# An encoder trunk on one core: C tables loaded behind three quarters of the scan inputs, first weights on ACT's queue, the gelu table load and the third in-chunk product moved in their queues

## The chip, the core and the metric

One core of a Trainium2 chip runs the whole program. The metric is device time in microseconds for one execution, the median of the runs. TensorE is PE in the rows, Vector DVE, Scalar ACT, GpSimd POOL; SP issues most of the DMAs, ACT some.

## The reference, cut to what matters

Two layers of an encoder over 512 tokens of width 1024, float32. Layer 0 mixes tokens with a bidirectional diagonal state-space model, layer 1 with a gated short convolution; each layer then attends into 256 memory tokens and applies a squared-ReLU MLP. The change lies wholly in layer 0's mixer:

```python
u = (h @ w_in)                         # 64 groups of 16 channels
y = d * u
for r in range(2):                     # two directions
    a_bar = exp(lam * dt)              # 64 states per group, complex
    bu = einsum('gph,lbgh->lbgp', b_bar, u)
    states = scan(x[l] = a_bar * x[l-1] + bu[l])
    y = y + einsum('ghp,lbgp->blgh', c, states).real
z = gelu(y); z = z * sigmoid(z @ w_glu); out = z @ w_out
```

## The kernel before, in words

The dense products of the program run as three float32r products on TensorE, fed by a stream of 1 MB weight blocks. Ahead of them, up to some 217 us of 1466, stands the mixer of layer 0, which is scheduled by hand: between `tc.manual_schedule()` and its end each engine executes its instructions in the order in which the code names them, so the order of the calls is the order of each queue.

The 512 tokens are cut into 64 chunks of 8. The mixer then has these steps, with the helper that holds each:

- `win_mm` (L683): u = x times `a_w_in`, four blocks of 256 columns. The loop at L253 to L258 loads x in four pieces (`xp`) and the first weight block in four pieces (`win[0]`), by turns on SP; ACT scales each x piece by the norm's gain (L276). `u_evac` (L690, L692) multiplies by the norm's factor on DVE, writes to DRAM and reads it back as `U` in the chunk layout.
- `sf_step`, `sf_transpose` (L518, L519): tables that carry a chunk's inputs into the state, eight of them (two per block of u), made on DVE, transposed on TensorE, copied by ACT to `sf`. They need the B tables `bf`.
- `s_mats` (L532, L534), eight calls, the "scan inputs": U times sf on TensorE, copied by ACT into `estate`, the state array of 64 chunk ends.
- `c_load` (L271): two transfers of 512 KB, the real and imaginary C tables `cf[0]` and `cf[1]`, on SP, and a page for their sum. `act.mul(cf[1], cf[1], -1.0)` (L747) negates the imaginary one on ACT. `q_tables` then forms the sum `cs` of both on DVE, and `q_ops` the eight Q tables (five DVE instructions each), which carry states to outputs.
- `scan_run`: the 62 scan steps on DVE, four small instructions a step, the last four Q tables woven between the first steps.
- `strips` (L556 to L576), four calls: in-chunk weights from Q and C tables on TensorE, copied by ACT (L570, L571), written to DRAM and read back by eight transfers as `mt` on SP. `y_intra(i)` (L586) is the in-chunk product of quarter i: U times mt. `y_carry` (L593) adds Q times the carried state.
- `p_part` (L673, L674): copies the states from `estate` into `pt`, for y_carry, in three portions as the scan goes on: chunks 0 to 26 and 26 to 46 on ACT, the rest mostly on DVE.
- `kvp(n)` runs n of the matmuls that make the memory's keys (L646) and values (L648) for layer 0. They fill TensorE while DVE scans; ACT copies the results (L658, L662). Their eight weight blocks are loaded on ACT's queue (four) and on SP's.

Pages of 4 KB a partition come from one pool of 30 (`page`): a new tile takes the buffer of a released one and waits for that one's last reader.

ACT loads its table of functions twice here: for the square root at the start (L89) and for gelu (L808), each with a one-column activation that fetches it ahead of its use.

Of the kernel before, what the change touches and what calls it, by code (L numbers as in the profile page):

```python
# [15 lines left out]
AF = mybir.ActivationFunctionType  # L16
# [30 lines left out]
def tile_encoder(ctx, tc, xT, xN, memT, memN, small, b_re, b_im, c_re, c_im, a_w_in, a_w_glu,  # L47
                 a_w_out, b_w_in, b_w_out, x_w_q, x_w_kv, x_w_o, f_w1, f_w2, out):
    nc = tc.nc
    v = nc.vector  # L50
    act = nc.scalar
# [15 lines left out]
    def nm(s):  # L67
        uid[0] += 1
        return f"{s}_{uid[0]}"

    def page(shape, dt=F32, name="pg"):
        return pgpool.tile([P] + list(shape), dt, tag="pg", name=nm(name))

    def bank(shape, name="ps"):
        return pspool.tile([P] + list(shape), F32, tag="ps", name=nm(name))
# [10 lines left out]
    epsb = cpool.tile([P, 1], F32, name="epsb")  # L86
    nc.gpsimd.memset(epsb, EPS)
    warm = cpool.tile([P, 1], F32, name="warm")
    act.activation(warm, epsb, AF.Sqrt)  # L89

    def gain(vec, k):
        o = OFF_G + vec * KT + k
        return sm[:, o:o + 1]
# [4 lines left out]
    def wblock(w, c0, k0=0):  # L98
        return w[k0 * P:(k0 + KT) * P, c0:c0 + 256].rearrange("(k p) m -> p k m", p=P)
# [152 lines left out]
    win = [stpool.tile([P, KT, 256], F32, tag="st", name=nm("st"))]  # L252
    w0 = wblock(a_w_in, 0)  # L253
    for kp in range(4):
        xp = xbig[:, 2 * kp:2 * kp + 2, :]
        nc.sync.dma_start(out=xp, in_=xT[256 * kp:256 * kp + 256, :].rearrange("(k p) n -> p k n", p=P))
        nc.sync.dma_start(out=win[0][:, 2 * kp:2 * kp + 2, :], in_=w0[:, 2 * kp:2 * kp + 2, :])
        hn.append(xp)  # L258
    bf = [page([G, 16], F32, "bf") for _ in range(2)]
    nc.sync.dma_start(out=bf[0], in_=b_re)  # L260
# [5 lines left out]
    cf = []  # L266

    def c_load():
        for src in (c_re, c_im):
            cf.append(page([G, 16], F32, "cf"))  # L270
            nc.sync.dma_start(out=cf[-1], in_=src)  # L271
        cf.append(page([G, 16], F32, "cs"))

    for k in range(KT):
        xk = hn[k // 2][:, k % 2, :]
        act.activation(xk, xk, AF.Copy, scale=gain(G_MIX, k))  # L276
# [35 lines left out]
    def tt(o, a, b, op):  # L312
        v.tensor_tensor(out=o, in0=a, in1=b, op=op)  # L313
# [139 lines left out]
    def q_tables():  # L453
        tt(dd, sm[:, OFF_D:OFF_D + 16].unsqueeze(2).to_broadcast([P, 16, 16]),
           sm[:, OFF_PAT:OFF_PAT + 16].unsqueeze(1).to_broadcast([P, 16, 16]), ALU.mult)
        tt(eq2[0], eq[:, 1], eq[:, 0], ALU.subtract)
        tt(eq2[1], eq[:, 0], eq[:, 1], ALU.add)
        tt(cf[2], cf[0], cf[1], ALU.add)
# [37 lines left out]
    def sf_gen(b):  # L496
        res, ops = gen_ops(b, bf, bs, es, [es2[:, 0], es2[:, 1]], False, "sfT")
        run_ops(ops)
        sfT[b] = res

    def bb_copy(b):
        res = sfT[b]
        for ri in range(2):
            o = bb[:, ri, 128 * b:128 * b + 128].rearrange("p (g h) -> p g h", g=8)
            act.copy(o[0:64], res[ri][0:64, :, :, 7])
            act.copy(o[64:128], res[ri][64:128, :, :, 0])
# [3 lines left out]
    def sf_transpose(b):  # L510
        outp = []
        for ri in range(2):
            pg = page([8, P], F32, "sf")
            for hb in range(2):
                ps = bank([4, P], "tr")
                for i in range(4):
                    g = 4 * hb + i
                    pe.transpose(ps[:, i, :], sfT[b][ri][:, g].rearrange("p h j -> p (h j)"), ident)  # L518
                act.copy(pg[:, 4 * hb:4 * hb + 4, :], ps)  # L519
            outp.append(pg)  # L520
        sf[b] = outp
# [3 lines left out]
    def s_mats(b):  # L525
        for ri in range(2):
            ps = bank([NC, 8], "ps_s")
            for g in range(8):
                u = U[b // 2][:, 8 * (b % 2) + g, :]
                for r in range(2):  # L530
                    rs = slice(64 * r, 64 * r + 64)
                    pe.matmul(ps[rs, :, g], lhsT=sf[b][ri][:, g, rs], rhs=u[:, ::-1] if r else u,  # L532
                              start=True, stop=True)
            act.copy(estate[:, 1:NC, ri, 8 * b:8 * b + 8], ps[:, 0:NC - 1, :])  # L534
# [46 lines left out]
    def y_intra(i):  # L581

        yps[i] = [(fbank if i == 3 else bank)([4, P], "y") for _ in range(2)]
        for g in range(8):
            for b2 in range(2):
                pe.matmul(yps[i][g // 4][64 * b2:64 * b2 + 64, g % 4, :], lhsT=U[i][:, 8 * b2 + g, :],  # L586
                          rhs=mts[i][:, 8 * b2 + g, :], start=(g % 4 == 0), stop=False)
# [80 lines left out]
    def p_part(b, s0, s1, engs):  # L668

        if b not in pts:  # L670
            pts[b] = page([2, 8, NC], F32, "pt")
        e = estate[:, s0:s1, :, 8 * b:8 * b + 8].rearrange("p s r g -> p r g s")
        engs[0](pts[b][0:64, :, :, s0:s1], e[0:64])  # L673
        engs[1](pts[b][64:128, :, :, NC - s1:NC - s0], e[64:128][:, :, :, ::-1])  # L674
# [4 lines left out]
    def win_mm(i, ms=(0, 1)):  # L679
        for k, m in [(k, m) for k in range(KT) for m in ms]:  # L680
            if (i, m) not in ups:
                ups[i, m] = bank([S], "u")
            pe.matmul(ups[i, m], lhsT=win[i][:, k, m * P:(m + 1) * P], rhs=hn[k // 2][:, k % 2, :],  # L683
                      start=(k == 0), stop=(k == KT - 1))
# [12 lines left out]
    def kv_load(i):  # L697
        kvst[i] = stage_load(wblock(x_w_kv[0], 256 * i), act if 2 <= i < 6 else None)
# [3 lines left out]
    def kvp(n):  # L702
        for _ in range(n):
            next(kv_it, None)

    def sf_step(b):
        sf_gen(b)
        bb_copy(b)
# [26 lines left out]
    sf_step(4)  # L735
    u_evac(2)
    win_mm(3, (1,))
    c_load()
    kv_load(0)
    kv_load(1)  # L740
    sf_transpose(2)
# [2 lines left out]
    nc.gpsimd.memset(estate[:, 0], 0.0)  # L744
    s_mats(0)
    s_mats(1)
    act.mul(cf[1], cf[1], -1.0)  # L747
    sf_step(6)
    u_evac(3)
    sf_transpose(4)  # L750
    s_mats(2)
    s_mats(3)
    sf_step(7)
    sf_transpose(5)
    s_mats(4)
# [2 lines left out]
    sf_transpose(7)  # L758
    s_mats(6)
    s_mats(7)  # L760
    q_tables()
    for b in range(4):
        run_ops(q_ops(b))
# [4 lines left out]
    def scan_run(n, extra=()):  # L768

        extra = list(extra)  # L770
        for i in range(n):
            for j in range(4):
                tt(*sc[ns[0]])
                ns[0] += 1
                if j >= 2 and extra:
                    tt(*extra.pop(0))
        run_ops(extra)
# [11 lines left out]
    scan_run(3, q_ops(7))  # L789
    y_intra(1)  # L790
    mts[3] = strips(3, 2)
    kvp(8)
    scan_run(14)
    y_intra(2)
    kvp(8)
    for b in range(4):
        p_part(b, 0, 26, (act.copy, act.copy))
    kvp(16)
# [4 lines left out]
    for b in range(4):  # L803
        p_part(b, 26, 46, (act.copy, act.copy))
    kvp(16)
    for b in range(4, 8):
        p_part(b, 26, 46, (act.copy, act.copy))
    act.activation(warm, epsb, AF.Gelu_apprx_tanh)  # L808
    scan_run(62 - 46)


# [424 lines left out]
```

## Time and profile before

| | |
|---|---|
| median of 3 runs | 1467.41 us (1466.83 to 1467.73) |
| the profiled execution's own time | 1467.9 us |
| its span, first to last instruction | 1466.0 us |
| TensorE busy | 1431.0 us, 98% |
| DVE busy | 863.6 us, 59% |
| ACT busy | 544.0 us, 37% |
| DMA | 155.50 MB, mean 106 GB/s |

Busy time is an average over stages that are bound by different things: up to 217 us the mixer, where several engines feed each other, then the dense part, where TensorE runs without gaps. What a change in the mixer is worth is read from the waits and the order of time there, not from these shares.

### The profile page before, as it was taken

What the parts mean: (1) busy time and instruction counts of PE and PEld (TensorE: products, weight loads), DVE (VectorE), ACT (ScalarE), POOL (GpSimd) and SP (SyncE); (2) the same over time, 40 slices, a digit from 0 to 9 for tenths busy, and PEclk for the clock granted to TensorE, in tenths of its full rate; (3) what the DMA queues carried; (4) which work ended last, traced back from release to release, by engine and by line L of the source; (5) the groups of instructions that cost most, each with busy time, mean ns of one, the idle gap of its engine ahead of it and who ended that gap; (6) DMA issues with size and microseconds to landing.
All of it is one profiled execution on the core that took longest, in us unless ns stands there. A gap on an engine that the chain in (4) does not pass through costs nothing.

```text
span 1466.0 us, 19448 instructions
## 1 busy us (share of the span) xinstructions
PE 1431.0 (98%) x8146; PEld 1179.3 (80%) x8146; DVE 863.6 (59%) x1362; ACT 544.0 (37%) x816; POOL 0.9 (0%) x10
## 2 busy tenths in 40 slices
PE   7999869999999999999999999999999999999997
PEld 3587768888888888888888889988888888888886
DVE  8799984766665444444367546456666544444435
ACT  4660574544443132322234224333444323132221
POOL 0000000000000000000000000000000000000000
PEclk9999989999999999999999999999999999999999
DMA  8626633322134223233133224522024323323201
GB/s 293 186 61 186 173 108 111 118 81 72 58 115 143 88 90 112 86 97 105 58 102 100 86 87 152 194 86 87 30 86 148 111 86 99 103 87 114 87 1 58
DMA packets 157304, 155.50 MB, mean 106 GB/s; under 512 B 11424, under 2 KB 152864, under 8 KB 157216
## 3 DMA queue, kind: packets, MB, share of 16 engines
q1 hardware_dynamic: 151968, 149.01, 32.0%
q10 hardware_dynamic: 5248, 5.24, 1.2%
q8 instruction: 64, 1.05, 0.3%
q14 instruction: 24, 0.20, 0.0%
HBM read 148.08 MB, written 6.16 MB: 105 GB/s over the span
## 4 chain that ended last, share of the span: by engine, by line
PE 95%; ACT 2%; DMA 2%; SPq 1%; issue 1%; DVE 0%; DVEq 0%; ACTq 0%
PE lin L166 26%; PE lin L167 26%; PE lin L168 26%; PE u L683 4%; PE kv L648 2%; PE y L593 1%; PE kv L168 1%; PE kv L167 1%; PE kv L166 1%; PE ps_s L532 1%; DMA mt<-wd 1%; PE kv L646 1%; PE tr L518 1%; SPq L576 1%; DMA wd<-wt 1%; PE sc L168 1%
## 5 line engine op out<-in xcount | busy, mean ns | idle before, releaser
L144 DVE TENSOR_TENSOR wl<-st,wh 128x1024 fp32r<-128x1024 f32 x224 | 270.5, 1222 | 178.8 <-ACT wh L143 174.9
L143 ACT CAST wh<-st 128x1024 fp32r<-128x1024 f32 x224 | 231.3, 1049 | 324.8 <-PE lin L167 291.5
L166 PE MATMUL lin<-hnh,wh 128*128 128x512 f32 x832 | 326.0, 392 | 0.0
L168 PE MATMUL lin<-hnh,wl 128*128 128x512 f32 x832 | 323.7, 389 | 0.0
L167 PE MATMUL lin<-hnl,wh 128*128 128x512 f32 x832 | 323.7, 389 | 0.0
L166 PE MATMUL lin<-mid,wh 128*128 128x512 f32 (+1 forms) x528 | 202.4, 383 | 0.0
L168 PE MATMUL lin<-mid,wl 128*128 128x512 f32 (+1 forms) x528 | 202.0, 383 | 0.0
L167 PE MATMUL lin<-mid,wh 128*128 128x512 f32 (+1 forms) x528 | 202.0, 383 | 0.0
L166 PEld LDWEIGHTS lin<-hnh,wh 128*128 128x128 f32 x832 | 156.2, 188 | 33.4 <-issue 1.2
L167 PEld LDWEIGHTS lin<-hnl,wh 128*128 128x128 f32 x832 | 156.2, 188 | 33.3 <-issue 1.2
L168 PEld LDWEIGHTS lin<-hnh,wl 128*128 128x128 f32 x832 | 156.2, 188 | 32.6
L166 PEld LDWEIGHTS lin<-mid,wh 128*128 128x128 f32 x528 | 99.2, 188 | 19.4
L168 PEld LDWEIGHTS lin<-mid,wl 128*128 128x128 f32 x528 | 99.2, 188 | 19.4
L167 PEld LDWEIGHTS lin<-mid,wh 128*128 128x128 f32 x528 | 99.2, 188 | 19.3
L313 DVE TENSOR_TENSOR relu<-relu,lin 128x512 f32<-128x512 f32 x64 | 43.7, 683 | 104.4 <-ACT relu L1020 104.4
L313 DVE TENSOR_TENSOR mo<-lin,r 128x512 f32<-128x512 f32 (+1 forms) x66 | 44.2, 675 | 101.8 <-PE lin L168 101.6
L1020 ACT ACTIVATE relu<-lin 128x512 f32<-128x512 f32 x64 | 38.0, 594 | 128.2 <-PE lin L168 127.8
L879 ACT ACTIVATE hnh<-h,sm 128x512 fp32r<-128x512 f32 x40 | 28.7, 718 | 125.8 <-DVE h L313 120.2
L683 PE MATMUL u<-xbig,st 128*128 128x512 f32 x128 | 57.8, 611 | 7.7 <-DMA st<-in_a_w_in_dram 7.7
L313 DVE TENSOR_TENSOR h<-lin,h 128x512 f32<-128x512 f32 x32 | 21.9, 691 | 61.3 <-PE lin L168 61.3
L683 PEld LDWEIGHTS u<-xbig,st 128*128 128x128 f32 x128 | 24.9, 196 | 38.2 <-issue 37.3
L1022 ACT CAST mid<-relu 128x512 fp32r<-128x512 f32 x64 | 39.6, 618 | 42.5 <-DVE relu L313 41.8
(219 smaller groups left out, 1939.3 us busy)
## 6 DMA issues: line engine op xcount, KB each, us to landing
st<-in_f_w_dram SPq DMA_DIRECT2D x64, 1024.0 KB, 5.7
st<-in_x_w_kv_dram SPq DMA_DIRECT2D x12, 1024.0 KB, 5.3
st<-in_b_w_in_dram SPq DMA_DIRECT2D x12, 1024.0 KB, 5.1
st<-in_x_w_q_dram SPq DMA_DIRECT2D x8, 1024.0 KB, 5.3
st<-in_x_w_o_dram SPq DMA_DIRECT2D x8, 1024.0 KB, 5.2
mt<-wd SPq DMA_DIRECT2D x32, 128.0 KB, 3.4
st<-in_x_w_kv_dram ACTq DMA_DIRECT2D x4, 1024.0 KB, 7.4
st<-in_a_w_glu_dram SPq DMA_DIRECT2D x4, 1024.0 KB, 5.5
```

Of the source, the lines that this page charges most:

```text
L143: act.copy(hi, src)
L144: v.tensor_tensor(out=lo, in0=src, in1=hi, op=ALU.subtract)
L166: pe.matmul(ps, lhsT=wh, rhs=xh, start=start, stop=False)
L167: pe.matmul(ps, lhsT=wh, rhs=xl, start=False, stop=False)
L168: pe.matmul(ps, lhsT=wl, rhs=xh, start=False, stop=stop)
L313: v.tensor_tensor(out=o, in0=a, in1=b, op=op)
L518: pe.transpose(ps[:, i, :], sfT[b][ri][:, g].rearrange("p h j -> p (h j)"), ident)
L648: pe.matmul(ps[:, m, :], lhsT=mk[:, ms], rhs=st[:, k, :], start=(k == 0), stop=(k == KT - 1))
L683: pe.matmul(ups[i, m], lhsT=win[i][:, k, m * P:(m + 1) * P], rhs=hn[k // 2][:, k % 2, :], start=(k == 0), stop=(k == KT - 1))
L879: act.activation(a.hi(k), hk(k), AF.Copy, scale=gain(vec, k))
L1020: act.activation(r_, ps[m], AF.Relu)
L1022: act.copy(md[:, k, 0, :], r_)
```

## The change

It touches the order of issue alone; no instruction is added or taken away but for the DMAs that change their queue.

```diff
-    act.activation(warm, epsb, AF.Sqrt)
...
         nc.sync.dma_start(out=xp, in_=xT[...])
-        nc.sync.dma_start(out=win[0][:, 2 * kp:2 * kp + 2, :], in_=w0[...])
+        act.dma_start(out=win[0][:, 2 * kp:2 * kp + 2, :], in_=w0[...])
...
+    act.activation(warm, epsb, AF.Sqrt)
     for k in range(KT):
         act.activation(xk, xk, AF.Copy, scale=gain(G_MIX, k))
...
     win_mm(3, (1,))
-    c_load()
     kv_load(0)
     kv_load(1)
...
     s_mats(0)
     s_mats(1)
-    act.mul(cf[1], cf[1], -1.0)
     sf_step(6)
     u_evac(3)
     sf_transpose(4)
     s_mats(2)
     s_mats(3)
+    c_load()
     sf_step(7)
...
     s_mats(6)
     s_mats(7)
+    act.mul(cf[1], cf[1], -1.0)
     q_tables()
...
     mts[3] = strips(3, 2)
-    kvp(8)
+    act.activation(warm, epsb, AF.Gelu_apprx_tanh)
     scan_run(14)
-    y_intra(2)
-    kvp(8)
+    kvp(16)
...
     for b in range(4):
         p_part(b, 26, 46, (act.copy, act.copy))
     kvp(16)
+    y_intra(2)
     for b in range(4, 8):
         p_part(b, 26, 46, (act.copy, act.copy))
-    act.activation(warm, epsb, AF.Gelu_apprx_tanh)
     scan_run(62 - 46)
```

On ACT, in the stage of the scan inputs, before (`estate` rows are the copies of s_mats, `cf` the imaginary C table, `bb` and `sf` tables of the next scan inputs):

```order
L534 COPY estate<-ps_s_619 128x63x8
L534 COPY estate<-ps_s_637 128x63x8
L747 ACTIVATE cf_511<-cf_511 128x1024
L505 COPY bb<-sfT_656 64x128
L506 COPY bb<-sfT_656 64x128
```

and in the changed program, where the negation is line 760 (`wt` is the first strip):

```order
L519 COPY sf_920<-tr_927 128x512
L534 COPY estate<-ps_s_933 128x63x8
L534 COPY estate<-ps_s_951 128x63x8
L534 COPY estate<-ps_s_969 128x63x8
L534 COPY estate<-ps_s_987 128x63x8
L760 ACTIVATE cf_768<-cf_768 128x1024
L570 COPY wt_1289<-w_275_1166 128x4x128
```

The negation stood behind the second of the eight scan inputs and now stands behind the last, with 36 more of ACT's instructions ahead of it. DVE's order is the same as before in this stage.

On SP in the same stage, in the changed program (`ud` and `U` are the write and the read of the fourth block of u, `st` weight blocks, `wd` the first strip):

```order
L102 DMA st_509<-in_x_w_kv_dram 128x8x256
L102 DMA st_511<-in_x_w_kv_dram 128x8x256
L690 DMA ud<-ut_662 128x2x512
L692 DMA U_666<-ud 128x16x64
L270 DMA cf_766<-in_c_re_dram 128x1024
L270 DMA cf_768<-in_c_im_dram 128x1024
L572 DMA wd<-wt_1289 128x4x240
```

The two C transfers stood ahead of the two weight blocks, and now stand behind the fourth block of u.

At the start of ACT's queue, as a difference (`st` is the first weight block, four pieces):

```order
-L89 ACT_TABLE_LOAD
-L89 ACTIVATE warm<-epsb 128x1
+L1229 UNCONDITIONAL_BRANCH
+L256 DMA st_91<-in_a_w_in_dram 128x2x256 x4
+L273 ACT_TABLE_LOAD
+L273 ACTIVATE warm<-epsb 128x1
 L276 ACTIVATE xbig<-xbig,sm 128x512 x8
```

The four weight pieces left SP's queue and stand ahead of the table load on ACT's.

## Rows read from the trace of the kernel before

**Rows 1.** The page, chain of work that ended last: shares of the span by engine.

```profile
PE 95%; ACT 2%; DMA 2%; SPq 1%; issue 1%; DVE 0%; DVEq 0%; ACTq 0%
```

**Rows 2.** Busy time by stretch: stretch, its length, PE, PEld, DVE, ACT, POOL, PEclk, DMA, GB/s.

```profile
7.00:8.00 1.00, 0.30 (x1) 0.34 (x2) 0.93 (x7) 0.00 (x0) 0.00 (x0) 1.00 1.05 378
80.00:100.00 20.00, 19.91 (x499) 18.54 (x498) 19.97 (x20) 18.03 (x37) 0.00 (x0) 1.00 0.18 49
```

**Rows 3.** Chain in order of time, the start: start us, us, what.

```profile
1.65 5.91 DMA st<-in_a_w_in_dram
...
7.70 12.55 PE u L683 x24
```

**Rows 4.** Timeline of ACT, the start: start us, us, instructions, idle time ahead.

```profile
0.73 1.28 ACT L89 ACT_TABLE_LOAD   x1 [0.73 <-PEq L1226]
...
4.92 1.33 ACT L276 ACTIVATE xbig<-xbig,sm 128x512 f32<-128x512 f32 x2 [2.70 <-DMA xbig<-in_xT_dram]
```

**Rows 5.** Chain in order of time, 68 to 100 us.

```profile
79.54 1.06 ACT cf L747
...
94.72 3.88 PE ps_s L532 x128
```

**Rows 6.** Timeline of DVE, the sum of the C tables.

```profile
85.88 1.22 DVE L313 TENSOR_TENSOR cs<-cf,cf 128x1024 f32<-128x1024 f32 x1
```

**Rows 7.** Timeline of ACT, the last copy of the scan inputs.

```profile
98.65 0.58 ACT L534 COPY estate<-ps_s 128x504 f32<-128x504 f32 x1 [0.35 <-PE ps_s L532]
```

**Rows 8.** Timeline of PE, the scan inputs.

```profile
74.94 3.95 PE L532 MATMUL ps_s<-U,sf 128*64 128x64 f32 x128 [1.45 <-ACT sf L519]
...
80.72 4.26 PE L532 MATMUL ps_s<-U,sf 128*64 128x64 f32 x128
```

**Rows 9.** SP's queue at 60 to 85 us, then DMA issues: KB, us to landing.

```profile
63.10 1.15 SPq L271 DMA_DIRECT2D cf<-in_c_re_dram  x1
...
81.57 0.37 SPq L692 DMA_DIRECT2D U<-ud  x1
...
cf<-in_c_re_dram SPq DMA_DIRECT2D x1, 512.0 KB, 6.7
...
st<-in_x_w_kv_dram SPq DMA_DIRECT2D x12, 1024.0 KB, 5.3
```

**Rows 10.** Timeline of ACT, the end of the scan.

```profile
195.28 1.28 ACT L808 ACT_TABLE_LOAD   x1
...
196.80 3.03 ACT L674 COPY pt<-estate 64x288 f32<-64x288 f32 x5
```

**Rows 11.** Timeline of PE, 148 to 200 us.

```profile
155.78 3.29 PE L586 MATMUL y<-mt,U 128*64 128x128 f32 x32 [4.15 <-issue]
159.00 24.44 PE L648 MATMUL kv<-st,mem 128*128 128x256 f32 x112
...
197.53 9.81 PE L593 MATMUL y<-Q,pt 128*64 128x128 f32 x128 [6.13 <-ACT pt L674]
```

**Rows 12.** Timeline of DVE, the scan's last writes and the copies behind it.

```profile
194.89 0.61 DVE L313 TENSOR_TENSOR estate<-estate,sc 128x128 f32<-128x128 f32 x2
...
196.40 0.48 DVE L674 COPY pt<-estate 64x288 f32<-64x288 f32 x1
```

**Rows 13.** SP's queue, the loads of the last two value blocks.

```profile
162.75 7.28 SPq L103 DMA_DIRECT2D st<-in_x_w_kv_dram  x2
```

**Rows 14.** Timelines of DVE and PE: last Q table's end, the fourth strip's third quarter.

```profile
141.29 1.22 DVE L313 TENSOR_TENSOR Q<-gt,Q 128x1024 f32<-128x1024 f32 x1
...
144.27 0.61 PE L556 MATMUL w<-Q,bb 64*32 64x112 f32 x32
```

**Rows 15.** Timeline of ACT, value and state copies: first and last portion.

```profile
163.48 0.92 ACT L673 COPY pt<-estate 64x416 f32<-64x416 f32 x1
...
181.75 0.84 ACT L662 ACTIVATE V<-kv,rmc 128x256 f32<-128x256 f32 x2 [2.61 <-PE kv L648]
...
183.99 0.75 ACT L673 COPY pt<-estate 64x320 f32<-64x320 f32 x1
```

More of the change, by code (lines that the diff above doesn't have):

```diff
@@ L256, in tile_encoder @@
         nc.sync.dma_start(out=xp, in_=xT[256 * kp:256 * kp + 256, :].rearrange("(k p) n -> p k n", p=P))
-        nc.sync.dma_start(out=win[0][:, 2 * kp:2 * kp + 2, :], in_=w0[:, 2 * kp:2 * kp + 2, :])
+        act.dma_start(out=win[0][:, 2 * kp:2 * kp + 2, :], in_=w0[:, 2 * kp:2 * kp + 2, :])
         hn.append(xp)
```

## The prediction

> **What bounds the kernel now.** I read the chain of waits first, since it says which engine ends last: TensorE holds 95% of it [rows 1], most of that in the dense part, which this change does not touch. The change lives in the mixer ahead of it, so I went on with busy time by stretch. Vector (DVE) is busy 19.97 of 20 us from 80 to 100 us [rows 2], and the view of waits lists not one wait of DVE's between 80 and 196 us; what it is short of full later is the small gap between scan operations that depend on each other. TensorE waits in that time, 4.15 us at once and 6.13 at the end [rows 11]. So the reader should see two stages. Up to 98.6 us TensorE sets the pace (input projection, transposes, scan inputs). From 85.88 us to 195.50 us [rows 6, 12] DVE does, without a hole: sum of the C tables, four Q tables, then 62 scan steps with four more Q tables between them. What makes DVE start that run later makes the kernel end later, one for one, unless something behind it has been slower still.
>
> **Part 1, the start.** The first matmul runs at 7.70 us; what let it go was the first quarter of the first weight block, issued on SP at 1.65 us and landed 5.91 us later [rows 3]. In the change the four weight pieces are issued by ACT, the first as its first instruction. ACT's first instruction of before began at 0.73 us, so the piece can leave 0.92 us sooner, and the four x pieces no longer stand between weight pieces. The upper bound is the other operand: ACT scales x at 4.92 us, 1.33 us for two, so half of that is done at 5.59 [rows 4], and TensorE could not start before: 2.1 us gained. The lower bound is nothing, if the weights land when they did. I take 1.4 us: the upper bound, less 0.7 us for the 256 KB of weights that now share the engines with the first x piece at the 378 GB/s which they reach at 7 to 8 us [rows 2]. The table load (1.28 us) now stands behind four issues on ACT, some 0.5 us each as on SP, and in front of the scaling at 4.92; it ends near 4 us and costs nothing; were it late, the lower bound covers it. The Trainium skill has a rule that speaks against this part: its page "DMA: Bandwidth & Descriptors", section "Issuing engines are not separate DMA queues", says that transfers begun on several engines run on the same 16 DMA engines and save only the issuing time. By that rule the gain would be the 0.92 us of issue, and the sum below 12.7 in place of 12.2 us; no row of before shows two queues at once at the start.
>
> TensorE works back to back to 70 us, so this 1.4 us reaches the stage of the scan inputs.
>
> **Part 2, the C tables: the term that decides.** Before, the two C transfers were issued from 63.10 us [rows 9], ACT negated the imaginary one at 79.54 us (1.06 us) in the middle of the scan inputs [rows 5], and DVE took the sum of both at 85.88 us without waiting [rows 6]. Now the transfers go out behind the fourth U load and the negation stands behind the last copy of the scan inputs on ACT. DVE's order is unchanged: the sum of the tables stands where it stood, with every Q table, every scan step and every later DVE instruction queued behind it. So it now waits for ACT's last scan input.
>
> When is that? The last copy of the scan inputs begins at 98.65 us and takes 0.58 [rows 7], so it ends at 99.23. It comes 1.4 us earlier by part 1. The negation no longer delays ACT in the middle; the chain goes through it, so 1.06 us is the bound for that gain. But TensorE's rows show how little of it was waited for: the 128 records across the negation, from 80.72 us, took 4.26 us, where 128 of the same kind took 3.95 from 74.94 [rows 8]. I take the difference, 0.3 us. Hence: last copy ends at 99.23 - 1.4 - 0.3 = 97.53, the negation ends 1.06 us later with 0.02 of hand-over, at 98.61, and DVE starts at about 98.66 instead of 85.88: **12.8 us later**.
>
> The loads do not set this: the fourth U load was issued at 81.57 us, the C transfers follow it and landed in 6.7 us each before [rows 9], so they are in by about 90 us. DVE's own inputs come earlier, too (three pages fewer are held while the tables of 64 to 84 us are made), but that only lengthens the wait at the sum. Who waits for DVE? TensorE for Q tables, with gaps from about 97 to 105 us, and ACT for TensorE; both had slack later.
>
> **Part 3, the gelu table load.** Before it ran at 195.28 us for 1.28 us, between ACT's copies of the state, and held the copy that begins at 196.80 [rows 10]; TensorE started the carry products at 197.53 [rows 11], 2.03 us after the scan's last write at 195.50. In the change it runs early, while ACT idles for TensorE. Then the carry products wait for DVE's copies instead: the one that began at 196.40 and took 0.48 us [rows 12] ends 1.38 us after the scan. The gain is 0.6 us (2.03 against 1.4), at least 0.
>
> **Part 4, the third in-chunk product.** It moves on TensorE behind the memory key and value products. Before, TensorE stood idle 4.15 us ahead of it, waiting for its transposed strip; the 112 records behind it take 24.44 us and could have run [rows 11]. That work was not what the scan waited for, so I cost the move itself at nothing; the cover is DVE's scan. What is late next is the last pair of value blocks: their loads sit on SP's queue behind the eight transfers of the fourth strip, and were issued from 162.75 us [rows 13]. The fourth strip's third quarter needs the last Q table: DVE ended it at 142.51 us, TensorE took it up at 144.27 [rows 14], so 1.8 of the 12.8 us are slack there, and these loads go out 11.0 us later, near 173.7. With 5.3 us to land [rows 9], 7.0 us for a block of 32 records, 1.3 us for the lower clock after idling (the 32 records of the product at 155.78 took 3.29 us; the same 32 for the quarter before it, at 138.54 in the same timeline and without idling, 1.97) and 5.2 us for three quarters of the next block, ACT may continue at about 192.5. What it has left then are two copies of 0.92, two pairs of 0.84 and 16 copies of 0.75 us [rows 15], 15.5 us: it ends at 208.0, the scan at 195.50 + 12.8 = 208.3. That is nearly even, so the term is 0, with 3 us as its upper end if loads or clock slip.
>
> **The sum.** 12.8 - 0.6 + 0 = +12.2 us. The profiled execution took 1467.9 us (span 1466.0 and 1.9 around it), 0.5 over the median of the runs, 1467.41. Against that median: **1479.6 us**.
>
> **The rivals.**
> *A second bound takes over (ACT's copies).* The same delay, but value loads land late, ACT passes the scan's end and the carry products wait for ACT. For it: part 4 leaves it under 1 us of room, and SP's queue is in order. Against: TensorE's low clock may pass sooner. It decides from 1 us of slip on; at 3 us the sum is 15.2 and the time 1482.6; I let it run from 1481.5 to 1485.
> *The stage before shrinks.* The full 2.1 us at the start, and the 1.45 us that TensorE idles ahead of 74.94 [rows 8] closes: 12.8 - 0.7 - 1.45 - 0.6 = 10.0 and 1477.4 us. Against it: that idle time is ACT's copies, which stay.
> *Faster: the sum of tables is not held.* If the negation were done by 85.9 us, as in a program where ACT's copies of the scan inputs ended some 12 us earlier, DVE would start its run on time or sooner; it could win part 1 and part 3, 2.0 us, and the 0.3: 1465.1 us. The point from which it decides is an end of the scan inputs at about 85 us. Against it: from 74.94 us on TensorE has hardly a gap [rows 8], and its last 128 records run from 94.72 to 98.60 [rows 5]; 12 us are not there to be taken.
> *No change: slack swallows it.* DVE would need 12 us of waiting inside 86 to 196 us. The view shows none; but ACT and TensorE might have been slower than DVE in the end (ACT ended at 195.28). That they were both within 0.3 us of DVE does not give room for the delay; about 1467.
>
> **How the numbers follow.** Something over 0.2% (2.9 us) is what a measurement of this kernel can tell from no change. Forecast 0.74, ACT's copies 0.14, the shrinking stage 0.07: all slower, 0.95. Faster 0.03, no change 0.02. The range reaches down to the shrinking stage (1477.4) and up to part 1 at nothing with part 4 at 3 us (1479.6 + 1.4 + 3.0 = 1484.0), with half a us on either side, as the runs shown lie up to 0.9 us apart: 1476.9 to 1484.5.
>
> **What would show it.** In the profile after: the first matmul at about 6.3 us; no negation among the scan inputs; DVE's sum of the C tables at about 98.7 us with some 13 to 15 us idle ahead of it, released by ACT's negation; the scan's end near 208 us; no table load there and TensorE's carry products about 1.4 us behind it; then the dense part as before, 12 us later. The prediction would be wrong if DVE's sum of the tables ran before 90 us, if the scan ended before 200 us, or if the carry products began more than 3 us after it.

## The result and the profile after

| | before | after |
|---|---|---|
| median of 4 runs | 1467.57 us (1466.83 to 1468.28) | 1482.23 us (1481.57 to 1482.46) |
| ratio | | 1.0097, 95% interval 1.0084 to 1.0110 |
| profiled execution, its span | 1467.9, 1466.0 us | 1482.46, 1480.4 us |
| mean granted clock of TensorE | 0.992 | 0.987 |

The changed kernel is slower by 14.7 us of the medians, 14.4 of the spans; the forecast was 12.2. A ratio can differ a little from the quotient of two medians, here and below; where it does, the ratio with its interval is the one to go by. In the rows after, the negation is L760 and the gelu load L792; other lines stand as before or one off.

The chain of work that ended last, on the page of the kernel after, is still mostly TensorE's dense part, but DVE has 2% of it where it had 0% [rows 1]:

```profile
PE 94%; DVE 2%; ACT 2%; DMA 1%; SPq 0%; issue 0%; DVEq 0%; ACTq 0%
```

The view of waits, DVE from 55 to 225 us, after (line and what it waited for; us in total, times, longest):

```profile
DVE cs L313 <- ACT cf L760: 14.7, 1, 14.7
DVE sfT L313 <- PE tr L518: 4.5, 1, 4.5
```

The first line is new and is the result in one row: one wait, for ACT's negation, at the sum of the C tables. The chain in order of time shows how it comes about (start, us, what):

```profile
80.72 3.88 PE ps_s L532 x128
...
98.25 0.58 ACT estate L534
...
98.86 1.06 ACT cf L760
...
99.94 1.24 DVE cs L313
```

Last copy of the scan inputs, negation, sum: the sum stands at 99.94 us, 14.06 later than before [rows 6]. DVE's timeline carries that to the end of the scan without a change:

```profile
99.94 1.23 DVE L313 TENSOR_TENSOR cs<-cf,cf 128x1024 f32<-128x1024 f32 x1 [14.70 <-ACT cf L760]
101.27 1.23 DVE L313 TENSOR_TENSOR gt<-cs,eq 128x1024 f32<-128x1024 f32 x1
...
209.03 0.61 DVE L313 TENSOR_TENSOR estate<-estate,sc 128x128 f32<-128x128 f32 x2
```

From the first Q table's first instruction (101.27) to the scan's last write (209.03 + 0.61 = 209.64) it is 108.37 us. In the kernel before it was 195.50 - 87.13 = 108.37 as well, and in every kernel below it lies between 108.35 and 108.38. DVE's run is a block of fixed length; only its start moves.

At the start of the program the chain is released by x, no longer by the weights [rows 3, 4]:

```profile
1.18 5.68 DMA xbig<-in_xT_dram
...
6.95 0.73 ACT xbig L276
...
7.72 4.30 PE u L683 x5
```

The first matmul starts at 7.72 us, 0.02 later than before: the first piece of x was scaled at 4.92 and now at 6.95. Behind the scan, ACT's timeline (start, us, instruction, idle time ahead and what ended it) and TensorE's:

```profile
196.46 0.91 ACT L673 COPY pt<-estate 64x416 f32<-64x416 f32 x1 [12.67 <-PE kv L648]
...
211.10 3.67 ACT L674 COPY pt<-estate 64x320 f32<-64x320 f32 x6
```

```profile
182.60 15.55 PE L648 MATMUL kv<-st,mem 128*128 128x256 f32 x64 [5.80 <-DMA st<-in_x_w_kv_dram]
...
212.46 9.10 PE L593 MATMUL y<-Q,pt 128*64 128x128 f32 x128 [4.52 <-ACT pt L674]
```

The carry products start at 212.46, 2.82 us behind the scan's end; before it was 2.03 [rows 11, 12]. There is no table load in the way any more, but ACT's last copy of the second portion (64x320) begins at 211.10, after the scan is over, and the first copy of the third portion stands behind it. One early copy (64x416, of the last of the eight state blocks) had waited 12.67 us for TensorE.

### The profile page after: what moved, and what is told of

The parts are those of the page before. It is cut to its first block, busy times and chain, and to the rows that moved or that the text cites. A ratio compares the mean times of both kernels' runs of the same rounds, so it can differ in the third digit from the quotient of the medians.

```text
span 1480.4 us, 19449 instructions
## 1 busy us (share of the span) xinstructions
PE 1434.8 (97%) x8146; PEld 1180.1 (80%) x8146; DVE 863.5 (58%) x1362; ACT 544.2 (37%) x816; POOL 0.9 (0%) x10
## 4 chain that ended last, share of the span: by engine, by line
PE 94%; DVE 2%; ACT 2%; DMA 1%; SPq 0%; issue 0%; DVEq 0%; ACTq 0%
PE lin L165 26%; PE lin L167 26%; PE lin L166 25%; PE u L683 4%; PE kv L646 2%; DVE Q L313 1%; PE y L593 1%; PE ps_s L532 1%; PE kv L167 1%; PE kv L166 1%; PE kv L165 1%; PE kv L648 1%; PE tr L518 1%; PE sc L167 1%; PE sc L166 1%; PE sc L165 1%
```

## The experiments

One table first: where DVE's first Q table starts, where the scan ends, how far behind it the carry products start, and the time. The kernel before was run again beside each series; its medians there were 1468.69 us (15 runs, first four kernels), 1468.59 (27 runs, next four) and 1469.43 (35 runs, last four), wider spread (1466.2 to 1473.7) than in the first measurement, so single microseconds are read from ratios and traces. The first three columns come from one profiled execution of each kernel. The column "carry behind it" has 2.82 us with the weights alone moved and 2.03 in the kernel before, though both have the same order there: some 0.8 us of such a difference can be the execution's own.

| kernel | first Q | scan ends | carry behind it | median us | ratio to before |
|---|---|---|---|---|---|
| before | 87.13 | 195.50 | 2.03 | 1467.57 | |
| after | 101.27 | 209.64 | 2.82 | 1482.23 | 1.0097 (1.0084 to 1.0110) |
| after, tables back | 87.89 | 196.24 | 6.90 | 1468.6 | 1.0003 (0.9994 to 1.0012) |
| after, load back | 100.90 | 209.26 | 2.04 | 1482.31 | 1.0095 (1.0080 to 1.0110) |
| before, tables moved | 100.25 | 208.61 | 2.20 | 1480.87 | 1.0086 (1.0073 to 1.0100) |
| before, negation behind sixth | 95.15 | 203.53 | 1.69 | 1476.03 | 1.0050 (1.0038 to 1.0063) |
| before, weights on ACT | 86.48 | 194.84 | 2.82 | 1468.49 | 0.9999 (0.9989 to 1.0008) |
| before, gelu load early | 88.37 | 196.73 | 0.77 | 1466.88 | 0.9993 (0.9985 to 1.0002) |
| before, product late | 87.50 | 195.86 | 7.29 | 1472.04 | 1.0017 (1.0008 to 1.0026) |
| after, product back | 101.85 | 210.22 | 0.77 | 1480.8 | 1.0081 (1.0067 to 1.0095) |
| product late, two pages fewer | 86.82 | 195.20 | 0.77 | 1466.74 | 0.9981 (0.9972 to 0.9989) |
| three small tables early | 85.93 | 194.30 | 2.60 | 1467.18 | 0.9984 (0.9974 to 0.9994) |
| and the sum on GpSimd | 85.09 | 193.46 | 3.65 | 1467.65 | 0.9989 (0.9978 to 0.9999) |
| and two pages fewer | 86.88 | 195.25 | 0.77 | 1466.34 | 0.9977 (0.9968 to 0.9985) |

### Is it the C tables? Both of their moves undone

```diff
     win_mm(3, (1,))
+    c_load()
...
     s_mats(1)
+    act.mul(cf[1], cf[1], -1.0)
...
     s_mats(3)
-    c_load()
...
     s_mats(7)
-    act.mul(cf[1], cf[1], -1.0)
```

> The changed kernel with both the loading of the C tables and the negation back at their old places; the other three parts of the change stay. Theory (the whole delay is DVE's wait at the sum of the C tables): the sum stands at 85.2 to 85.9 us again instead of 99.94, the scan ends near 195.2, and the time falls by 14.06 us to about 1468.2. Rival one (weights on ACT's queue, product and gelu load cost something of their own, 2 us or more): 1470 us or above. Rival two (those parts gain what the forecast gave them at most): 1466.5 us or below.

Measured 1468.6 us, against 1468.69 of the kernel before in the same series. The delay is gone; the other three parts together come to nothing that the interval (0.9994 to 1.0012) can tell from zero. DVE's timeline has no wait ahead of the sum any more:

```profile
86.64 1.22 DVE L313 TENSOR_TENSOR cs<-cf,cf 128x1024 f32<-128x1024 f32 x1
```

That is 0.74 us later than the band expected. The profiled execution was the slowest of its eleven, 1473.34 us: there the carry products started 6.90 us behind the scan. That pointed at a cost of the third product, followed up below.

### The load or the negation? The load alone put back

```diff
     win_mm(3, (1,))
+    c_load()
...
     s_mats(3)
-    c_load()
```

> The changed kernel with the two C transfers alone back at their old place on SP; the negation stays behind the last scan input. Theory (ACT's order holds DVE, not the landing of the tables): the sum of the tables stays at 99.9 us behind a wait of over 13 us for ACT's negation, and the time at 1482 us, within 1. Rival (the later transfers on SP cost the time): the sum comes at 86 to 90 us and the time falls to 1468 to 1472.

1482.31 us, and DVE's timeline of this kernel has the same wait:

```profile
99.64 1.23 DVE L313 TENSOR_TENSOR cs<-cf,cf 128x1024 f32<-128x1024 f32 x1 [14.05 <-ACT cf L760]
```

The later transfers cost nothing that shows: the sum stands 0.30 us sooner than in the changed kernel, and the first matmul 0.37 (7.35 us here, 7.72 there). It is the place of one 1.06 us instruction in ACT's queue.

### The tables' move alone

```diff
-    c_load()
     kv_load(0)
...
     s_mats(1)
-    act.mul(cf[1], cf[1], -1.0)
...
     s_mats(3)
+    c_load()
...
     s_mats(7)
+    act.mul(cf[1], cf[1], -1.0)
```

> The kernel before with the C transfers and the negation moved as in the change, and nothing else. Theory: the sum at 99.9 us, 14.06 later than before, the scan's end 14.1 later, and nearly the whole difference, 1481.6 us. Rival (the copies behind a later third product make a second bound of their own): without that move 1.5 to 3 us less than the changed kernel, 1479.2 to 1480.7, or, if the gelu load between the copies costs its 0.6 us here as before, nearer the first figure.

1480.87 us, 12.2 over the kernel before in its series and 12.6 by the ratio. That is 0.73 us below "nearly the whole" and 0.17 above the band of the second account, so it is nearer to the second. By the ratios the tables carry some 12.6 of the 14.2 us (0.0086 and 0.0097 of 1467.57), but the two intervals overlap, so the rest is read from the runs on the product below. DVE's timeline:

```profile
98.92 1.23 DVE L313 TENSOR_TENSOR cs<-cf,cf 128x1024 f32<-128x1024 f32 x1 [14.70 <-ACT cf L760]
```

The sum stood 1.02 us sooner than in the changed kernel, and 0.73 of that is the first matmul (6.99 us here, 7.72 there).

### A smaller dose: the negation behind the sixth scan input

```diff
     s_mats(1)
-    act.mul(cf[1], cf[1], -1.0)
...
     s_mats(5)
+    act.mul(cf[1], cf[1], -1.0)
```

> The kernel before with the negation alone moved, behind the copies of the sixth scan input instead of the second; the C transfers stay where they were. A smaller dose of the same delay. Theory (one for one): those copies end between 93.0 and 94.0 us, the negation 1.06 later, so DVE's sum stands at 94.1 to 95.1 instead of 85.88, 8.2 to 9.2 us later, and the time is 1475.8 to 1476.8. Rival (some slack swallows part of a smaller delay): under 1474. Rival (the jump comes at once with any move): 1480 or over.

1476.03 us, in the band expected, though the sum was a little sooner than the band. DVE's timeline:

```profile
93.89 1.22 DVE L313 TENSOR_TENSOR cs<-cf,cf 128x1024 f32<-128x1024 f32 x1 [8.27 <-ACT cf L757]
```

8.01 us later than before [rows 6], the carry products 205.22 - 197.53 = 7.69 later, the time 7.3 over the kernel before in its series. With 14.06 us for the whole move, that is a line with a slope of about one: no slack swallows the smaller dose.

### The first weights on ACT's queue, alone

```diff
-        nc.sync.dma_start(out=win[0][...], in_=w0[...])
+        act.dma_start(out=win[0][...], in_=w0[...])
```

> The kernel before with the four pieces of the first weight block on ACT's queue, and nothing else. Theory (both queues fill the same 16 DMA engines, so the weights come sooner and the first piece of x later): ACT scales that piece at 6.5 to 7.0 us instead of 4.9 to 5.5, the first matmul starts at 7.3 to 7.7 us where the weights on SP gave 7.0 to 7.7, released by ACT, and the time is within 0.7 us of the kernel before. Rival (what the prediction took): first matmul at 6.3 us and 1.4 us less.

1468.49 us against 1468.59. ACT's timeline of this kernel, then TensorE's:

```profile
6.71 1.34 ACT L276 ACTIVATE xbig<-xbig,sm 128x512 f32<-128x512 f32 x2 [3.99 <-DMA xbig<-in_xT_dram]
```

```profile
7.49 29.27 PE L683 MATMUL u<-xbig,st 128*128 128x512 f32 x64 [7.49 <-ACT xbig L276]
```

Over all fourteen kernels: with the weights on ACT's queue (five of them) x was scaled at 6.57 to 6.95 us and the first matmul started at 7.35 to 7.72; with the weights on SP (nine) x at 4.92 to 6.54 and the matmul at 6.44 to 8.08. The means of the first matmul are 7.53 and 7.44 us. What one operand gains the other loses: in the changed kernel the first piece of the weights landed 3.9 us after its issue at 0.73, in the kernel before 5.91 after 1.65, so 2.9 us sooner; the first piece of x, issued at 1.18 in both, landed after 5.68 us in place of 3.7, so 2.0 later.

### The gelu table load, alone

```diff
     kvp(8)
+    act.activation(warm, epsb, AF.Gelu_apprx_tanh)
     scan_run(14)
...
-    act.activation(warm, epsb, AF.Gelu_apprx_tanh)
     scan_run(62 - 46)
```

> The kernel before with the gelu table load alone moved ahead of the fourteen scan steps. Theory (what the prediction took): the load ends in ACT's idle time, the carry products start 1.4 us behind the scan's end, now behind DVE's copies, instead of 2.0 to 2.2, and the time falls by 0.6 us to 0.8. Rival (ACT's copies behind the scan still end last): 2.0 us or more remain and no change.

DVE's last write of the scan, then TensorE's timeline:

```profile
196.12 0.61 DVE L313 TENSOR_TENSOR estate<-estate,sc 128x128 f32<-128x128 f32 x2
```

```profile
197.50 9.63 PE L593 MATMUL y<-Q,pt 128*64 128x128 f32 x128 [4.87 <-ACT pt L674]
```

The carry products start 197.50 - 196.73 = 0.77 us behind the scan's end, 1.26 sooner than in the kernel before, about the 1.28 us of the load. The time is 1466.88 us, 1.0 below the kernel before by the ratio and 1.7 by the medians, but the interval still holds 1: the gain is seen in the trace, not in the time.

### The third product, alone

```diff
     scan_run(14)
-    y_intra(2)
     kvp(8)
...
         p_part(b, 26, 46, (act.copy, act.copy))
     kvp(16)
+    y_intra(2)
     for b in range(4, 8):
```

> The kernel before with the third in-chunk product alone moved behind the memory values. Theory (the eighth early copy of the states has its page from the memory tokens instead of from what the product releases, waits for TensorE's last value products, and puts ACT's copies behind the scan): that copy begins only with 9 us or more of idle time ahead of it on ACT, ended by TensorE, the carry products start 3 us or more behind the scan's end instead of 2.0, and the time is 1 to 5 us above the kernel before. Rival (what the prediction took: the scan covers the move): no change within 0.7 us and the carry products 2.0 to 2.2 us behind the scan.

1472.04 us, 3.4 over the kernel before by the medians, 2.5 by the ratio (1.2 to 3.8 by its interval). So the move that the prediction costed at nothing is a loss when it stands alone. The profiled execution was the slowest of its eleven, 1473.07 us, so the trace shows the loss at its largest. ACT's timeline, then TensorE's:

```profile
185.57 0.92 ACT L673 COPY pt<-estate 64x416 f32<-64x416 f32 x1 [15.75 <-PE kv L648]
186.51 0.93 ACT L674 COPY pt<-estate 64x416 f32<-64x416 f32 x1
187.45 0.84 ACT L662 ACTIVATE V<-kv,rmc 128x256 f32<-128x256 f32 x2
```

```profile
170.55 16.72 PE L648 MATMUL kv<-st,mem 128*128 128x256 f32 x64 [6.99 <-DMA st<-in_x_w_kv_dram]
...
203.15 8.90 PE L593 MATMUL y<-Q,pt 128*64 128x128 f32 x128 [6.07 <-ACT pt L674]
```

The copy at 185.57 reads chunks that the scan had finished long before; it has nothing to do with the matmuls it waits for. It waits for its buffer: in the order of page requests it gets a page of the memory tokens, which the last value product still reads. The time fits that: the first of the two pages of memory tokens is read last when three quarters of the last block are done, 56 of these 64 records, which is at about 170.55 + 7/8 of 16.72 = 185.2 us. All of ACT's second portion, sixteen copies, queues behind it.

### The product back in its place, within the whole change

```diff
-    kvp(16)
+    kvp(8)
+    y_intra(2)
+    kvp(8)
...
     kvp(16)
-    y_intra(2)
```

> The changed kernel with the third in-chunk product alone back at its old place. Theory (the product's late place costs the 1.4 us by which the carry products started too late): the eighth early copy does not wait for TensorE, the carry products start 1.4 us behind the scan's end instead of 2.8, and the time is 1480.3 to 1481.0. Rival (the copies end late because the scan is late for them all): 2.8 us behind the scan's end and 1482.2 us as with the whole change.

1480.8 us. ACT is ahead of the scan again and waits for it, and the carry products start 210.99 - 210.22 = 0.77 us behind the scan's end. ACT's timeline, then TensorE's:

```profile
194.21 0.84 ACT L662 ACTIVATE V<-kv,rmc 128x256 f32<-128x256 f32 x2 [5.85 <-PE kv L648]
...
206.97 0.73 ACT L674 COPY pt<-estate 64x320 f32<-64x320 f32 x1
210.25 3.00 ACT L674 COPY pt<-estate 64x288 f32<-64x288 f32 x5 [2.55 <-DVE estate L313]
```

```profile
181.85 14.05 PE L648 MATMUL kv<-st,mem 128*128 128x256 f32 x64 [2.90 <-DMA st<-in_x_w_kv_dram]
...
210.99 9.15 PE L593 MATMUL y<-Q,pt 128*64 128x128 f32 x128 [7.15 <-ACT pt L674]
```

So of the 2.82 us in the changed kernel, 2.05 are the product's late place by these two traces, where 1.4 were expected. The size is rough: the kernel with the load alone back has the late product too, and 2.04 where the changed kernel has 2.82. In the time it is 1.4 us, with the scan's end 0.58 later here, and the two intervals overlap.

The wait itself does not go away with the product: ACT's third value copy stands behind 5.85 us of it. But it comes two copies of 0.92 us later in ACT's order than in the changed kernel, and it ends sooner (194.21 us against 196.46): TensorE goes on with the last two blocks at 181.85 in place of 182.60, and needs 14.05 us for them in place of 15.55. TensorE had been idle 2.90 us ahead of them, and 5.80 in the changed kernel, where the granted clock over them was 0.90 and here 1.00.

### The late product with two pages fewer wanted

```diff
         if b not in pts:
-            pts[b] = page([2, 8, NC], F32, "pt")
+            pts[b] = (bb[:, b - 6, 0:1024].rearrange("p (a g s) -> p a g s", a=2, g=8) if b >= 6
+                      else page([2, 8, NC], F32, "pt"))
```

This is laid over the run with the product alone moved. 

> The kernel before with the third product alone moved, as in the run that cost 3.4 us, but with the copies of the seventh and eighth state block kept in the bb buffer, which nothing reads any more by then, so that two pages fewer are wanted. Theory (what the late product costs, it costs through the pages: ACT's eighth early copy and its third value copy wait for pages of the memory tokens, which are read until the last value product): no early copy waits for TensorE, the third value copy goes some 7 us before the last, the second portion of copies ends before the scan, the carry products start at most 2.2 us behind the scan's end instead of 7.3, and the time is 3 us or more below that run, 1467 to 1469. Rival (the last value weights land late and TensorE is late for itself): the carry products stay 5 us or more behind the scan, and 1471 to 1472.

1466.74 us, 5.3 below that run and faster than the kernel before (0.9972 to 0.9989). ACT's timeline:

```profile
177.48 0.84 ACT L662 ACTIVATE V<-kv,rmc 128x256 f32<-128x256 f32 x2 [6.37 <-issue]
...
184.34 0.84 ACT L662 ACTIVATE V<-kv,rmc 128x256 f32<-128x256 f32 x2
...
191.19 1.28 ACT L809 ACT_TABLE_LOAD   x1
...
195.23 1.26 ACT L675 COPY pt<-estate 64x288 f32<-64x288 f32 x2 [2.54 <-DVE estate L313]
```

No early copy waits, the third value copy goes at 177.48 and the last at 184.34, and even the gelu load in its old place ends before the scan does (2.54 us of idle time for DVE behind it). TensorE still ran dry for 5.33 us ahead of the last value blocks, so the late weights alone are not what cost the time. They set how long the wait for a page lasts; that ACT waits at all comes from the pages. The kernel before seems to pay for them too: its third value copy stood at 181.75 behind 2.61 us of waiting for TensorE [rows 15], 4.27 us later than here, and its ACT ended at the scan's end.

### Further in the same direction: an earlier start for DVE

Three kernels over the early gelu load. The first moves the three small instructions ahead of the sum (`dd` and the two of `eq2`) in front of the sixth table of scan inputs:

```diff
     sf_transpose(2)
+    tt(dd, ...)
+    tt(eq2[0], eq[:, 1], eq[:, 0], ALU.subtract)
+    tt(eq2[1], eq[:, 0], eq[:, 1], ALU.add)
     sf_step(5)
```

> The kernel before with the gelu load early, and with three small DVE instructions of the Q tables (0.42 and 1.29 us in all) moved into the 5.1 us in which DVE idles for TensorE's transposes near 67 to 72 us. Theory (what starts DVE's run of Q tables and scan ends the mixer, one for one, in this direction too): the sum of the C tables stands 1.6 us sooner behind the first matmul, and the time is 1.6 us below that with the gelu load alone: 1465.2 to 1465.4 us. Rival (ACT's copies end only 0.2 us ahead of the scan there and bind next): 0.3 us below, 1466.6.

The second also gives the sum to GpSimd:

```diff
-        tt(cf[2], cf[0], cf[1], ALU.add)
+        nc.gpsimd.tensor_tensor(out=cf[2], in0=cf[0], in1=cf[1], op=ALU.add)
```

> As the run before it, and the sum of the C tables made by GpSimd instead of DVE. Theory: DVE's run is 1.22 us shorter still, and the time 1464.0 us if ACT's copies do not bind. Rival one (ACT's copies bind): no change against the run before it. Rival two (GpSimd takes over 4 us for the sum, or slows DVE while it runs): DVE waits for it ahead of the first Q table and the time rises.

The third adds the two pages to both.

> As the run before it, with the seventh and eighth state block in the bb buffer. Theory (ACT's copies are then held by pages and no more): ACT's second portion ends before the scan does, the carry products start 0.8 us behind the scan's end, and the time is 1464.0 us or below. Rival: the same time as the run before it, because the copies were not what bound it.

None reached the time that its theory gave: 1467.18, 1467.65 and 1466.34 us. In the first, DVE's first Q table starts 78.08 us behind the first matmul, where the kernel before has 79.43 and the early gelu load alone 80.50. So the sum did come sooner; but ACT then ends late and the carry products wait 2.60 us, which is what its rival says. The three instructions ran at 59.95 us, and did not fill the idle time at 67 to 72 us (4.9 us of it are left of 5.1) but a wait of 1.2 us for TensorE's `rb` ahead of it, which DVE's view of waits no longer has. In the second ACT's copies bind fully (the carry products start 3.65 us behind the scan), and the sum on GpSimd took so long that DVE waited, as its second rival has it. GpSimd's timeline, then DVE's:

```profile
79.08 5.97 POOL L454 TENSOR_TENSOR cs<-cf,cf 128x1024 f32<-128x1024 f32 x1 [10.37 <-ACT cf L747]
```

```profile
80.47 2.35 DVE L313 TENSOR_TENSOR sfT<-gt,sfT 128x1024 f32<-128x1024 f32 x2
85.09 1.23 DVE L313 TENSOR_TENSOR gt<-cs,eq 128x1024 f32<-128x1024 f32 x1 [2.26 <-POOL cs L454]
```

DVE saves 1.22 us and waits 2.26. The third takes ACT out of the way (0.77 us again) and keeps that loss; it has the lowest ratio of all, 0.9977 (0.9968 to 0.9985), but its interval overlaps that of the late product with two pages fewer. The three small tables with the pages and the sum on DVE might join the two gains; that was not tried.

## Why the prediction was right, and which steps failed

The sign and the term that decides were right: the load back alone, the tables back, the tables alone and the smaller dose all say that DVE waits for a negation behind ACT's last scan input, one for one. The forecast of 1479.6 us was 2.6 too low; the time lies in the range, and within the span given to the first rival, which had a chance of 0.14 against the forecast's 0.74. That is no luck of the range: its upper end was part 1 at nothing with part 4 at 3 us, and of that part 1 came at nothing and part 4 at some 2 us. What was luck is that 1.2 us came off unforeseen, 0.66 by a larger part 3 and 0.53 behind it (the sum stands below); without them the time would still lie in the range.

**Part 2** was right. Last copy of the scan inputs 0.40 us sooner (0.3 forecast), negation behind it, sum at 99.94 us. Without part 1 the working gives 12.8 + 1.4 = 14.2; measured 14.06.

**Part 1 failed: the step "the upper bound, less 0.7 us".** The forecast took 1.4 us; measured 0, its lower bound. It held the other operand at its old time, "ACT scales x at 4.92", while moving the weights ahead of it. In the changed kernel the first piece of x lands 2.0 us later, and the weights, 2.9 us sooner, wait for it. The rule that the prediction quoted from the Trainium skill, "DMA: Bandwidth & Descriptors", section "Issuing engines are not separate DMA queues", points the right way: by it the gain is the issue time, 0.92 us, and the runs show not even that.

**Part 3 was undersized: the step "the carry products wait for DVE's copies instead".** The gain alone is 1.26 us and not 0.6: the carry products started 0.77 us behind the scan, not 1.4. DVE's copy that was taken as the new limit was not.

**Part 4 failed: the steps "I cost the move itself at nothing" and "these loads go out 11.0 us later, near 173.7".** Its list of what ACT has left holds the two copies of 0.92 us, so the wait of the last early copy for TensorE was in the sum; but it was laid to the late loads and not to the move, which by the runs above makes it come two copies sooner. And it was sized too short. SP's queue in the kernel after, the loads of the last two value blocks:

```profile
176.11 1.16 SPq L102 DMA_DIRECT2D st<-in_x_w_kv_dram  x2
```

They went out 13.36 us later than before and not 11.0: 14.14 of the scan, of which 0.78 was slack and not 1.8. TensorE went on 6.49 us behind that (5.3 taken), and ACT at 196.46 (192.5 taken). From there the list held: ACT's second portion ends at about 211.8 and not at 208.0, the scan at 209.64 and not at 208.3, so ACT is 2.2 us late where the forecast had it 0.3 early. The upper end of 3 us held in the whole change. Alone, the move costs the carry products 7.29 - 2.03 = 5.26 us in the slowest execution and the time 2.5 us (1.2 to 3.8). The late scan hides a part: with the same late product and the tables back in their place the carry products start 6.90 us behind the scan, with the late scan 2.82.

So the rival "ACT's copies" came true, on top of a part 1 that gave nothing. From the traces the difference of the spans is 14.14 (scan's end) + 0.79 (carry products behind it) - 0.72 (from there to the first dense matmul, at 217.45 us before and 231.66 after: 19.92 and 19.20) + 0.19 (dense part) = 14.40 us, against 12.8 - 0.6 = 12.2. The 0.79 is part 4's 2.05 less part 3's 1.26. The 0.72 was not forecast: the first carry products ran faster, with a higher granted clock. Busy time by stretch over them, before and then after (columns as in rows 2):

```profile
197.50:207.30 9.80, 9.77 (x129) 9.60 (x129) 5.96 (x10) 5.59 (x8) 0.00 (x0) 0.72 0.01 2
```

```profile
212.50:221.50 9.00, 9.00 (x129) 8.83 (x129) 5.09 (x8) 5.54 (x8) 0.00 (x0) 0.79 0.01 2
```

The same 129 records at a mean granted clock of 0.72 and of 0.79, a mix of its two levels, 1.2 and 2.4 GHz. TensorE had been idle 6.13 us ahead of the first and 4.52 ahead of the second.

The rivals "the stage shrinks", "faster" and "no change" are out: the idle time ahead of the scan inputs stayed at 1.45 us, and DVE's run had the same 108.37 us.

## What to carry to other kernels

An instruction's place in an in-order queue can cost far more than its length: 1.06 us of work behind the wrong neighbours cost 14 us, since a gapless run of another engine starts with its result. When work is moved, ask whose buffers it releases and who gets them next; the copy that waited here for an engine whose results it does not use was waiting for a page, and wanting two pages fewer turned a move that lost time into one that gained. And when one of two operands is to arrive sooner, work out anew when the other one will.

## What the runs showed of the hardware

- A sum of two 128x1024 float32 tables took 5.97 us on GpSimd and 1.22 us on DVE, 4.9 times as long, and DVE's wait for it ended with it. DVE's own instructions beside it kept their length (two of 128x1024 in 2.35 us). The Trainium skill, "GPSIMD Engine Reference", section "4.1 Engine selection", speaks of about two times slower for operations with two inputs; 5.97 us differ from that. But DVE was busy beside the sum up to 82.82 us, and GpSimd ended at 85.05, only 2.23 us later, which is 1.8 times 1.22. Whether GpSimd worked all the 5.97 us or was held while DVE was busy is left open: no run has the sum on GpSimd beside an idle DVE.
- The first 256 KB of weights let the first matmul go anywhere from 6.44 to 8.08 us in nine kernels with the same order of transfers on SP. A gain of less than that spread, 1.6 us, at the start cannot be read from one profiled execution.
- Two 1 MB loads begun 0.71 us apart (176.11 and 176.82 us in the changed kernel) let TensorE go on at 182.60, 6.49 us behind the first; begun 3.39 us apart (175.59 and 178.98, the product back in its place), at 181.85, 6.26 us behind it. Beginning them together did not show as a cost for the first.
